# Three of eight experts with 64 slots, both parts of a token in one stationary tile, experts chosen by a register

## The chip, the cores and the metric

The kernel runs on one core of a Trainium2 chip. The number is the device time of one execution in microseconds (us). The engines named below are TensorE (PE, matmuls; PEld is its weight loads), VectorE (DVE), ScalarE (ACT), GpSimd (POOL) and SyncE (SP, which issues the transfers from HBM). Each takes its instructions in a fixed order; between engines there are semaphores.

## The reference

Two layers over 256 tokens of width 1024. The second layer ends in a mixture of experts, and the change is in that part alone:

```python
logits = (a @ w_r).astype(jnp.float32) + b_r.astype(jnp.float32)
top_v, top_i = lax.top_k(logits, TOP_K)          # 2 of 8 experts per token
gates = jax.nn.softmax(top_v, axis=-1)
...
ys = lax.map(lambda args: swiglu(args[0], w1[args[1]], w3[args[1]], w2[args[1]]), (xs, blk_exp))
# swiglu(a, w1, w3, w2) = (silu(a @ w1) * (a @ w3)) @ w2, inner width 2816
```

With the reference's inputs the router sends 47, 66, 93, 32, 81, 113, 59 and 21 tokens to experts 0 to 7.

## The kernel before

All arithmetic is float32. A float32 matmul is made of three faster ones on parts: each operand is split into a high part (rounded to the faster format, `float32r`) and a low part (the rest), and `mm3` (lines 173 to 176) adds high x high, low x high and high x low. The weights are split on the chip: a *unit* is 128 x 2048 floats, 1 MB of HBM, loaded by SP into one of ten raw buffers (`rw`, `rp`, `ra`, `rq`; class `Loads`, issue on line 49). ACT writes the high part (`wh`, line 80), DVE subtracts it from the raw unit (`wl`, line 84), and the raw buffer is free for the next transfer. There are three pairs of high and low buffers for the units of the experts (class `Parts`): `unit()` takes the next unit for TensorE, gives back the pair that TensorE used before it, and issues the splitting of the unit that goes into that pair. A unit of the experts is cast and subtracted in two halves of 1024 columns.

An expert has 11 chunks of 256 inner columns, and a chunk three units: two for w1 and w3 (`up`, 12 matmuls of 512 columns each, result `h`) and one for w2 (`down`, 12 matmuls, accumulated in `y`). Between them stand `act` (silu and product, tile `ga`) and `hidden` (two transposes into `ht`, then the high part `hh` on ACT and the low part `hl` on DVE). Each expert has 128 token slots, which are the 128 columns of the stationary tile. The tokens of a pair of experts are collected by one-hot matmuls (`gather`, during the odd expert before), and the outputs are weighted (`yh`, `yl`) and spread back into the token stream (`xl`, line 1206) in the expert that follows. In chunk g TensorE does `up` of g (with the transposes of g - 1 in its middle) and then `down` of g - 1. The order of all this is written out by hand. At the end a branch repeats an expert for tokens beyond slot 128; with the counts above it isn't taken.

The names of the prediction's steps: `Loads.advance` (45), `Parts.pump` (72), `up`, `act`, `hidden`, `down` (1159 to 1185), and the loop that calls them (1220 to 1272).

Of the kernel before, what the change touches and what calls it, by code (L numbers as in the profile page):

```python
# [34 lines left out]
NCH = FT // 2  # L35
LAM = 0.8 - 0.6 * math.exp(-0.3)


class Loads:
# [6 lines left out]
    def advance(self, most=99):  # L46
        while self.free and self.n < self.limit and most:
            t = self.free.popleft()
            self.nc.sync.dma_start(t, self.aps[self.n])
            self.got[self.n] = t  # L50
            self.n += 1
            most -= 1
# [11 lines left out]
class Parts:  # L64


    def __init__(self, nc, loads, engines, slots):
        self.nc, self.loads, self.engines, self.free = nc, loads, engines, deque(slots)
        self.got, self.n, self.cur, self.spent, self.left, self.holding = {}, 0, 0, [], [], False
        self.limit, self.last_use = len(loads.aps), None  # L70
# [39 lines left out]
    def release(self, most=99):  # L110

        self.holding = False
        keep = [self.spent.pop()] if self.left else []
        for n in self.spent:
            self.free.append(self.got.pop(n))
        self.spent = keep
        self.pump(most)
# [13 lines left out]
def backbone(ctx: ExitStack, tc: tile.TileContext, i, out):  # L131
# [18 lines left out]
    for e in range(NE):  # L150
        for c in range(NCH):
            units += [i["moe"][e, 3 * c], i["moe"][e, 3 * c + 1]]
            if e or c:
                e0, c0 = (e, c - 1) if c else (e - 1, NCH - 1)
                units.append(i["moe"][e0, 3 * c0 + 2])
    units.append(i["moe"][NE - 1, 3 * NCH - 1])
# [6 lines left out]
    def engines(u):  # L163

        if u >= 69:
# [4 lines left out]
    parts = Parts(nc, loads, engines, slots)  # L170
    aloads = Loads(nc, [i["ada"][l, u] for l in range(2) for u in range(24)], ada_slots)
# [722 lines left out]
    def routing(p):  # L894

        iota = p.tile([P, 2, P], F32, name="iota")
        PO.iota(iota.rearrange("p a s -> p (a s)"), pattern=[[1, 2 * P]], base=1, channel_multiplier=0,
                allow_small_or_imprecise_dtypes=True)
# [10 lines left out]
        f = {n: p.tile([P, 2, NE], F32, name=n) for n in ("lg", "rank", "posp", "gate")}  # L909
# [4 lines left out]
        f["cnt"] = p.tile([P, 1 + NE], F32, name="cnt")  # L914
        f["cnti"] = p.tile([P, 1 + NE], mybir.dt.int32, name="cnti")
# [137 lines left out]
    def onehot(t, pr, part):  # L1053

        for n in range(2):
            e = 2 * pr + n
            V.tensor_scalar(oh[t][:, n], r["iota"][:, part], r["posp"][:, t, e:e + 1], None, op0=OP.is_equal)
# [25 lines left out]
    for t in range(2):  # L1083
        onehot(t, 0, 0)
# [8 lines left out]
    def gates():  # L1093
# [5 lines left out]
        V.tensor_copy(r["cnt"][:, 1:], pp)  # L1099
# [7 lines left out]
        V.tensor_reduce(r["cnt"][:, 0:1], r["cnt"][:, 1:], axis=AX.X, op=OP.max)  # L1107
        V.tensor_copy(r["cnti"], r["cnt"])

    def gather():

        xs = [[xlo[:, b * D:(b + 1) * D].rearrange("p (k s) -> p k s", k=KT) for b in range(2)],
              [px.tile([P, KT, P], F32R, name=f"xs{b}", bufs=2) for b in range(2)]]
        late = None

        def low(x, k):
            for n in range(2):
                V.tensor_tensor(out=xs[n][1][:, k], in0=x[:, n], in1=xs[n][0][:, k].bitcast(F32), op=OP.subtract)  # L1120

        for k in range(KT):
# [11 lines left out]
            for n in range(2):  # L1134
                A.copy(xs[n][0][:, k], x[:, n])
# [23 lines left out]

    def up(ps, xs, h, w, ks=range(4)):  # L1160
        for k in ks:
            c = slice(k * T2, (k + 1) * T2)
            mm3(ps, xs[0][:, 4 * h + k], xs[1][:, 4 * h + k], w[0][:, c], w[1][:, c], h == k == 0, h == 1 and k == 3)

    def act(ps):
# [5 lines left out]
    def hidden(g):  # L1171
        pt = pst.tile([P, T], F32, name="ht")
        for f in range(2):
# [7 lines left out]
    def down(y, h, w, first, last):  # L1181
        for f, n in ((0, 0), (1, 0), (0, 1), (1, 1)):
            b = slice(f * P, (f + 1) * P)
            c = slice(f * D + n * T2, f * D + (n + 1) * T2)
            mm3(y[n], h[0][:, b], h[1][:, b], w[0][:, c], w[1][:, c], first and f == 0, last and f == 1)
# [33 lines left out]

    run, got, rets = gather(), {}, {}  # L1220
# [3 lines left out]
    last, res, parted = None, None, deque()  # L1224
    for e in range(NE):
        for c in range(NCH):
            n, pr = e % 2, e // 2
            ps = psh.tile([P, T2], F32, name="h13")
            w = parts.unit()
            for k in range(4):  # L1230
                if e == c == 0:
                    next(run)
                up(ps, got[pr][n], 0, w, [k])
                if k == 1 and last is not None:
                    h = hidden(last[2])
                    if res is not None:
                        parted.extend((m, w, res[2]) for m, w in enumerate(weighted(*res[:2])))
                        res = None
            if e == c == 0:
                next(run)  # L1240
                for _ in range(2):
                    parts.give(1)
                parts.holding = False
            if e == 0 and c == 1:
                gates()
            w = parts.unit()
            up(ps, got[pr][n], 1, w)
            g = act(ps)
            if parted:
                spread(*parted.popleft())  # L1250
            if last is not None:
                e0, c0, _ = last
                if c0 == 0:
                    y = acc()
                down(y, h, parts.unit(), c0 == 0, c0 == NCH - 1)
                if c0 == NCH - 1:
                    gs = rets[e0 // 2][1][:, e0 % 2:e0 % 2 + 1]
                    back = rets[e0 // 2][0][:, e0 % 2]
                    res = y, gs, back
# [126 lines left out]
```

## Time and profile before

| | |
|---|---|
| runs | 1630.42, 1634.49, 1636.94 us; median 1634.49 |
| profiled execution | 1633.3 us, of which the span is 1631.5 |
| experts, by the trace | from about 820 us to the end |
| busy over the span | PE 97%, PEld 80%, DVE 81%, ACT 55%, POOL 3% |
| granted TensorE clock | 0.985 of full speed |
| read from HBM | 397.87 MB, 264 units of the experts among it |

The span runs from the first to the last recorded instruction. A busy share is an average over stages with different limits, so the stage of the experts is looked at by itself. Ends of matmuls are modelled in the records; the distance from start to start of neighbours tells how fast they follow each other.

### The profile page before, as it was taken

Reading aid. Unit: us, or ns where it says so; the run is one execution under the profiler, and the core shown is the slowest. Engines: PE = TensorE matmul, PEld = TensorE weight load, DVE = VectorE, ACT = ScalarE, POOL = GpSimd, SP = SyncE. Lnnn points to the kernel's source line nnn. Section 1 sums busy time; section 2 is a strip of 40 time slices with the busy share of each in tenths; the row PEclk is TensorE's granted clock in tenths of the full one; section 3 lists DMA queues with packets and bytes.
Section 4 is the critical chain, followed back from the end, with each engine's and each line's share of the span. In section 5 each row is a group of like instructions: output and inputs, shape, how many; then the busy total and the mean of one; then the engine's idle time right before and its main releaser. Section 6 shows DMA issues by size and latency. Waiting matters only on the chain. (4 is left out here: it accounts for less than half of the span.)

```text
span 1631.5 us, 20995 instructions
## 1 busy us (share of the span) xinstructions
PE 1584.1 (97%) x7767; PEld 1307.2 (80%) x7767; DVE 1317.6 (81%) x1898; ACT 890.2 (55%) x1241; POOL 44.5 (3%) x157
## 2 busy tenths in 40 slices
PE   9899899999999999999899999999999999999997
PEld 7687689888888898887778888888888888888885
DVE  5888887758648667667578999989999899998986
ACT  3222244222222244445577778777777777877774
POOL 0000000000000002113000000000000000000000
PEclk9899999999999999999989999999999999999999
DMA  9245534545537514322459989999899999999890
GB/s 364 104 161 198 196 123 149 179 137 183 204 130 290 200 53 149 111 78 107 177 192 361 363 322 353 355 351 357 337 345 355 356 342 346 356 350 357 341 358 28
DMA packets 55728, 400.36 MB, mean 245 GB/s; under 512 B 6449, under 2 KB 6481, under 8 KB 7105
## 3 DMA queue, kind: packets, MB, share of 16 engines
q1 hardware_dynamic: 55298, 398.50, 65.0%
q8 instruction: 63, 1.03, 0.2%
q0 software_dynamic: 320, 0.44, 0.2%
q14 instruction: 47, 0.39, 0.1%
HBM read 397.87 MB, written 1.05 MB: 245 GB/s over the span
## 5 line engine op out<-in xcount | busy, mean ns | idle before, releaser
L84 DVE TENSOR_TENSOR wl<-rw,wh 128x1024 fp32r<-128x1024 f32 (+1 forms) x220 | 330.0, 1531 | 80.3 <-ACT wh L80 79.7
L80 ACT CAST wh<-rw 128x1024 fp32r<-128x1024 f32 (+1 forms) x219 | 276.9, 1296 | 63.3 <-PE mm L175 56.4
L174 PE MATMUL mm<-ah,wh 128*128 128x512 f32 (+1 forms) x576 | 222.4, 386 | 5.3 <-ACT ah L314 4.5
L176 PE MATMUL mm<-ah,wl 128*128 128x512 f32 (+1 forms) x576 | 221.2, 384 | 5.2 <-DVE wl L84 5.2
L175 PE MATMUL mm<-al,wh 128*128 128x512 f32 (+1 forms) x576 | 221.5, 384 | 0.0
L84 DVE TENSOR_TENSOR wl<-rp,wh 128x1024 fp32r<-128x1024 f32 (+1 forms) x160 | 192.9, 1246 | 19.7 <-ACT wh L80 19.7
L254 DVE SCALAR_TENSOR_TENSOR junk<-ra,cb 128x1024 bf16<-128x1024 f32 x136 | 166.3, 1223 | 3.3
L80 ACT CAST wh<-rp 128x1024 fp32r<-128x1024 f32 (+1 forms) x160 | 164.9, 1069 | 4.5 <-PE y L176 3.1
L174 PE MATMUL h<-wh,xl 128*128 128x512 f32 x352 | 144.7, 411 | 0.2 <-ACT wh L80 0.2
L175 PE MATMUL h<-wl,xl 128*128 128x512 f32 x352 | 140.9, 400 | 1.8 <-DVE wl L84 1.8
L174 PE MATMUL h<-wh,xs 128*128 128x512 f32 x352 | 142.7, 405 | 0.0
L176 PE MATMUL h<-wh,xl 128*128 128x512 f32 x352 | 140.0, 398 | 0.0
L174 PE MATMUL y<-wh,hh 128*128 128x512 f32 x352 | 138.9, 395 | 0.5 <-ACT hh L1177 0.5
L176 PE MATMUL y<-wh,hl 128*128 128x512 f32 x352 | 139.2, 396 | 0.0
L175 PE MATMUL y<-wl,hh 128*128 128x512 f32 x352 | 139.1, 395 | 0.0
L175 PE MATMUL h<-wl,xs 128*128 128x512 f32 x352 | 139.0, 395 | 0.0
L176 PE MATMUL h<-wh,xs 128*128 128x512 f32 x352 | 139.0, 395 | 0.0
L176 PEld LDWEIGHTS mm<-ah,wl 128*128 128x128 f32 x576 | 110.7, 192 | 27.9 <-DVE wl L84 7.2
L174 PEld LDWEIGHTS mm<-ah,wh 128*128 128x128 f32 x576 | 110.6, 192 | 27.6 <-ACT ah L314 5.3
L84 DVE TENSOR_TENSOR wl<-rq,wh 128x1024 fp32r<-128x1024 f32 x104 | 122.1, 1219 | 8.9 <-ACT wh L80 8.9
L84 DVE TENSOR_TENSOR wl<-ra,wh 128x1024 fp32r<-128x1024 f32 x104 | 122.5, 1220 | 8.2 <-ACT wh L80 6.9
L175 PEld LDWEIGHTS mm<-al,wh 128*128 128x128 f32 x576 | 110.8, 192 | 21.5 <-DVE al L309 0.9
(290 smaller groups left out, 2921.4 us busy)
## 6 DMA issues: line engine op xcount, KB each, us to landing
rw<-moe SPq DMA_DIRECT2D x81, 1024.0 KB, 5.0
rp<-moe SPq DMA_DIRECT2D x79, 1024.0 KB, 5.1
rw<-w SPq DMA_DIRECT2D x61, 1024.0 KB, 4.8
ra<-moe SPq DMA_DIRECT2D x52, 1024.0 KB, 4.9
rq<-moe SPq DMA_DIRECT2D x52, 1024.0 KB, 5.3
ra<-ada SPq DMA_DIRECT2D x44, 1024.0 KB, 4.9
rx<-ada SPq DMA_DIRECT2D x4, 1024.0 KB, 19.7
rp<-w SPq DMA_DIRECT2D x4, 1024.0 KB, 6.3
```

Source lines behind the costliest of these rows:

```text
L80: self.nc.scalar.copy(hi[:, c0], raw[:, c0])
L84: engine.tensor_tensor(out=lo[:, c], in0=raw[:, c], in1=hi[:, c].bitcast(F32), op=OP.subtract)
L174: PE.matmul(ps, wh, xh, start=first, stop=False)
L175: PE.matmul(ps, wh, xl, start=False, stop=False)
L176: PE.matmul(ps, wl, xh, start=False, stop=last)
L254: V.scalar_tensor_tensor(junk, raw[:, a * D:(a + 1) * D], 1.0, cb[:, s], op0=OP.mult, op1=OP.mult, accum_out=m[:, a, s:s + 1])
```

## The change

Experts 2 to 7 are put in an order on the chip, by their numbers of tokens (`places_of`): the three that have the fewest take places 2, 4 and 6 (`FEW`). Since the order is known only on the chip, SP reads it into registers (`choose`) and adds a register to the address of each of the 198 transfers of places 2 to 7.

A place in `FEW` has 64 slots. The high parts of its tokens stand in columns 0 to 63 of one stationary tile and the low parts in 64 to 127, so that a piece of weights takes two matmuls (times the high and the low weights, `two`) instead of three. The result has both parts' products in different partitions; `act` only copies it to SBUF (`hs`), and `hidden` adds the two by a matmul with a folding matrix (`fold`, four matmuls of 64 columns), then does silu, the product (`hg`) and the split. The units of these places are cast and subtracted whole, in one instruction of 2048 columns. In every third chunk (1, 4, 7, 10 of 0 to 10) the second unit isn't split at all (`whole`): TensorE multiplies the raw unit in plain float32, and its raw buffer is given back only when TensorE is done.

For all experts `down` comes one chunk later: chunk g does `up` with its first unit, `down` of g - 2, `hidden` of g - 1, `up` with its second unit, `act`. The units are loaded in that order. An expert's weighting and spreading move by as much. The branch at the end is taken beyond slot 64 for places in `FEW`.

```diff
     def pump(self, most=99, between=None):
-        while self.free and self.n in self.loads.got and self.n < self.limit and most:
+        while self.n in self.loads.got and self.n < self.limit and most and (self.free or self.n in self.whole):
             raw = self.loads.take(self.n)
+            if self.n in self.whole:
+                self.got[self.n] = raw, None
+                self.n += 1
+                continue
...
+    def moe_unit(e, u):
+        if e < 2:
+            return i["moe"][e, u]
+        return lambda: i["moe"][bass.ds(chosen[e - 2], 1), u].rearrange("a p c -> (a p) c")
...
-        if u >= 69:
+        if u >= 69 and u not in few:
             return [(c, [(V, c)]) for c in (slice(0, 1024), slice(1024, U))]
         return [(ALL, [(V, ALL)])]
...
+    def two(ps, x, w, c, first, last):
+        if w[1] is None:
+            PE.matmul(ps, x.bitcast(F32), w[0][:, c], start=first, stop=last)
+        else:
+            for b in range(2):
+                PE.matmul(ps, x, w[b][:, c], start=first and b == 0, stop=last and b == 1)
...
+    def act(ps, few=False):
+        if few:
+            g = px.tile([P, T2], F32, name="hs")
+            A.copy(g, ps)
+            return g
...
+    def hidden(g, few=False):
         pt = pst.tile([P, T], F32, name="ht")
+        if few:
+            for f in range(4):
+                PE.matmul(pt[:, f * H:(f + 1) * H], g[:, f * P:(f + 1) * P], fold, start=True, stop=True)
+            g = px.tile([P, P], F32, name="hg")
+            A.activation(g, pt[:, :P], AF.Silu)
+            V.tensor_tensor(out=g, in0=pt[:, P:], in1=g, op=OP.mult)
+            hb = px.tile([P, T], F32R, name="hh").rearrange("p (f b s) -> p f b s", f=2, b=2)
+            g = g.rearrange("p (f s) -> p f s", f=2)
+            A.copy(hb[:, :, 0], g)
+            V.tensor_tensor(out=hb[:, :, 1], in0=g, in1=hb[:, :, 0].bitcast(F32), op=OP.subtract)
+            return [hb]
...
+    for g, (e, c) in enumerate(chunks):
+        n, pr, few_now = e % 2, e // 2, e in FEW
+        ps = psh.tile([P, T2], F32, name="h13")
+        w = parts.unit()
+        for k in range(4):
...
+            up(ps, got[pr][n], 0, w, [k])
...
+        if g > 1:
+            y = finish(g - 2)
...
+        if g > 0:
+            hids[g - 1] = hidden(acts.pop(g - 1), chunks[g - 1][0] in FEW)
...
+        w = parts.unit()
+        for k in range(4):
+            up(ps, got[pr][n], 1, w, [k])
...
+        acts[g] = act(ps, few_now)
```

What the change does to the order of instructions is shown at expert 2 (place 2 after the change), on three engines. On ACT, one chunk of that expert before (`wh` are casts, `hh` and `ga` belong to the hidden values; what an instruction waits for stands in brackets):

```order
L1167 ACTIVATE ga<-h_8185 128x256 [waits DVE_49,PE_49]
L80 CAST wh_76<-rw_71 128x1024 [waits DMAHW5_49,DVE_49]
L80 CAST wh_76<-rw_71 128x1024 [waits DVE_49]
L80 CAST wh_78<-rp_4396 128x1024 [waits DMAHW6_49,DVE_49,PE_49]
L80 CAST wh_78<-rp_4396 128x1024 [waits DVE_49,PE_49]
L1177 CAST hh<-ht 128x256 [waits DVE_49,PE_49]
```

And on ACT, of the changed kernel, from the end of chunk 2 to the end of chunk 5 of place 2 (`hs` is the copy in `act`, `hg` the silu):

```order
L1251 COPY hs<-h_8242 128x512 [waits PE_49,Activation_49]
L88 CAST wh_74<-rp_4397 128x2048 [waits DMAHW0_49]
L88 CAST wh_76<-ra_70 128x2048 [waits DMAHW1_49,PE_49,Activation_49]
L1264 ACTIVATE hg<-ht 128x128 [waits DVE_49,PE_49]
L1268 CAST hh<-hg 128x2x64 [waits DVE_49]
L88 CAST wh_78<-rw_72 128x2048 [waits DMAHW2_49,Activation_49]
...
L88 CAST wh_74<-rw_73 128x2048 [waits DMAHW7_49,PE_49,Activation_49]
L1264 ACTIVATE hg<-ht 128x128 [waits DVE_49,PE_49]
L1268 CAST hh<-hg 128x2x64 [waits DVE_49]
L88 CAST wh_76<-rp_4396 128x2048 [waits DMAHW0_49]
L1251 COPY hs<-h_8421 128x512 [waits PE_49,Activation_49]
```

The cast `hh` now waits for DVE (the product `hg`), where it waited for TensorE, and one weight cast of each chunk stands behind it. The last five rows are a chunk after an unsplit unit, which has two weight casts instead of three. On DVE, one chunk of that expert before (`wl` are the subtractions of the weights):

```order
L84 TENSOR_TENSOR wl_77<-rp_4395,wh_76 128x1024 [waits DMAHW3_49,Activation_49]
L84 TENSOR_TENSOR wl_77<-rp_4395,wh_76 128x1024 [waits Activation_49]
L84 TENSOR_TENSOR wl_79<-rw_73,wh_78 128x1024 [waits DMAHW4_49,Activation_49]
L84 TENSOR_TENSOR wl_79<-rw_73,wh_78 128x1024 [waits Activation_49]
L1178 TENSOR_TENSOR hl<-ht,hh 128x256 [waits Activation_49]
```

Nothing of ACT waits for `hl` here. On DVE, chunk 3 of place 2 after:

```order
L92 TENSOR_TENSOR wl_75<-rq_6527,wh_74 128x2048 [waits DMAHW4_49,Activation_49]
L92 TENSOR_TENSOR wl_77<-rq_6528,wh_76 128x2048 [waits DMAHW5_49,PE_49,Activation_49]
L1265 TENSOR_TENSOR hg<-ht,hg 128x128 [waits Activation_49]
L1269 TENSOR_TENSOR hh<-hg,hh 128x2x64 [waits Activation_49]
L92 TENSOR_TENSOR wl_79<-rw_71,wh_78 128x2048 [waits DMAHW6_49,Activation_49]
```

The product `hg`, which ACT's `hh` waits for, stands behind two subtractions of 2048 columns. On TensorE, a stretch of chunk 3 of place 2 after: the end of `down`, the fold, and the start of the second `up`.

```order
L1237 MATMUL y_8253<-wh_78,hh 128x512
L1237 MATMUL y_8253<-wl_79,hh 128x512
L1262 MATMUL ht<-fold,hs 128x64 [waits Activation_49]
L1262 MATMUL ht<-fold,hs 128x64 x3
L1237 MATMUL h_8303<-wh_74,xl_5950 128x512 [waits Activation_49]
L1237 MATMUL h_8303<-wl_75,xl_5950 128x512 [waits DVE_49]
```

Each piece of weights has two matmuls where it had three, the fold has taken the place of two transposes, and the second matmul of a unit already needs the low part of the weights.

## Rows read from the trace of the kernel before

**Rows 1.** Windows: length, busy PE, PEld, DVE, ACT, POOL, clock, DMA, GB/s.

```profile
1000.00:1100.00 100.00, 100.00 (x460) 81.27 (x459) 92.20 (x110) 77.09 (x100) 0.00 (x0) 1.00 0.91 352
```

**Rows 2.** TensorE's longest wait from 820 us on: total, times, longest.

```profile
PE h L175 <- DVE wl L84: 1.8, 1, 1.8
```

**Rows 3.** Timeline of TensorE, one chunk of expert 2: start, length, instruction.

```profile
1104.52 0.39 PE L174 MATMUL h<-wh,xl 128*128 128x512 f32 x1
...
1105.69 0.39 PE L176 MATMUL h<-wh,xl 128*128 128x512 f32 x1
...
1106.37 0.40 PE L175 MATMUL h<-wl,xl 128*128 128x512 f32 x1
...
1113.13 0.39 PE L174 MATMUL h<-wh,xl 128*128 128x512 f32 x1
```

**Rows 4.** Timeline of DVE, weighting of the outputs of experts 0, 1, 2.

```profile
935.36 1.40 DVE L1193 SCALAR_TENSOR_TENSOR yl<-y,gs,yh 128x512 fp32r<-128x512 f32 x2
...
1036.01 1.40 DVE L1193 SCALAR_TENSOR_TENSOR yl<-y,gs,yh 128x512 fp32r<-128x512 f32 x2
...
1134.00 1.41 DVE L1193 SCALAR_TENSOR_TENSOR yl<-y,gs,yh 128x512 fp32r<-128x512 f32 x2
```

**Rows 5.** Timeline of TensorE, matmuls in plain float32.

```profile
720.86 1.05 PE L852 MATMUL o<-rp,wT 128*128 128x128 f32 x8
721.66 0.48 PE L174 MATMUL mm<-wh,ah 128*128 128x512 f32 x1
...
805.78 1.85 PE L1029 MATMUL o<-wrg,xl 128*128 128x8 f32 x16
```

**Rows 6.** Groups by form, whole run, ACT.

```profile
L80 ACT CAST wh<-rw 128x2048 fp32r<-128x2048 f32 x63 | 119.4, 1904 | 59.7 <-PE mm L175 56.4 <-PE mm L176 3.3
...
L475 ACT COPY cs<-mm 128x512 f32<-128x512 f32 x8 | 4.6, 579 | 0.0
...
L854 ACT ACTIVATE ojunk<-o 128x128 f32<-128x128 f32 x16 | 4.6, 285 | 6.9 <-PE o L852 6.8
```

**Rows 7.** Timelines of ACT and DVE in the first layer, two stretches.

```profile
287.82 0.62 ACT L564 CAST hh<-cs 128x512 fp32r<-128x512 f32 x1 [6.66 <-DVE cs L563]
288.35 1.91 ACT L80 CAST wh<-rw 128x2048 fp32r<-128x2048 f32 x1
...
341.13 1.91 ACT L80 CAST wh<-rw 128x2048 fp32r<-128x2048 f32 x1 [9.25 <-PE mm L175]
...
343.07 2.29 DVE L84 TENSOR_TENSOR wl<-rw,wh 128x2048 fp32r<-128x2048 f32 x1 [0.83 <-ACT wh L80]
345.28 1.22 DVE L254 SCALAR_TENSOR_TENSOR junk<-ra,cb 128x1024 bf16<-128x1024 f32 x1
```

**Rows 8.** Groups by form, whole run: busy, mean ns | idle before, DVE.

```profile
L84 DVE TENSOR_TENSOR wl<-rw,wh 128x2048 fp32r<-128x2048 f32 x64 | 146.3, 2290 | 67.1 <-ACT wh L80 67.1
...
L1206 DVE SCALAR_TENSOR_TENSOR xl<-g,mod,xl 128x256 f32<-128x256 f32 x64 | 26.5, 479 | 0.1
...
L729 DVE TENSOR_TENSOR qz<-mm,rope 128x128 f32<-128x128 f32 x32 | 7.1, 284 | 6.6 <-ACT qsq L717 6.5
```

**Rows 9.** Timeline of TensorE, second chunk of expert 0.

```profile
834.39 0.69 PE L1174 MATMUL ht<-ident,ga 128*128 128x128 f32 x2 [0.94 <-DVE ga L1168]
```

**Rows 10.** Timeline of TensorE, waits with a slow stretch behind them.

```profile
149.28 0.50 PE L176 MATMUL mm<-ah,wl 128*128 128x512 f32 x1 [1.83 <-DVE wl L84]
...
150.33 0.63 PE L174 MATMUL mm<-ah,wh 128*128 128x512 f32 x1
150.76 0.63 PE L175 MATMUL mm<-al,wh 128*128 128x512 f32 x1
...
153.73 0.39 PE L176 MATMUL mm<-ah,wl 128*128 128x512 f32 x1
```

**Rows 11.** Windows of TensorE: length, busy, clock, DMA, GB/s.

```profile
172.00:176.00 4.00, 1.55 (x7) 1.00 0.00 0
```

**Rows 12.** Windows: the last columns are clock, DMA share and GB/s.

```profile
16.00:20.00 4.00, 4.00 (x20) 4.00 (x21) 3.06 (x8) 2.00 (x4) 0.00 (x0) 1.00 1.01 424
```

More of the change, by code (lines that the diff above doesn't have):

```diff
@@ L35 @@
 NCH = FT // 2
+FEW = (2, 4, 6)
+H = P // 2
 LAM = 0.8 - 0.6 * math.exp(-0.3)
@@ L1184, in down @@
             c = slice(f * D + n * T2, f * D + (n + 1) * T2)
-            mm3(y[n], h[0][:, b], h[1][:, b], w[0][:, c], w[1][:, c], first and f == 0, last and f == 1)
+            a = first and f == 0, last and f == 1
+            if len(h) == 1:
+                two(y[n], h[0][:, f].rearrange("p b s -> p (b s)"), w, c, *a)
+            else:
+                mm3(y[n], h[0][:, b], h[1][:, b], w[0][:, c], w[1][:, c], *a)
     def weighted(y, g):
@@ L1223, in backbone @@
     parts.holding = True
[L1224 to L1239, printed above, removed]
-                next(run)
[L1241 to L1259, printed above, removed]
-            if n == 0 and c == 4:
-                rets[pr] = returns(pr)
-            if n == 1 and e < NE - 1:
-                if c == 1:
-                    for t in range(2):
-                        onehot(t, pr + 1, 0)
-                    run = gather()
-                if 2 <= c < 2 + KT:
-                    got[pr + 1] = next(run)
-            last = e, c, g
@@ L1270, in backbone, with finish @@
-    h = hidden(g)
-    down(y, h, parts.unit(), False, True)
+    res, parted, acts, hids, y = None, deque(), {}, {}, None
+    def finish(g):
+        result = y
+        e, c = chunks[g]
+        if c == 0:
+            result = acc()
+        down(result, hids.pop(g), parts.unit(), c == 0, c == NCH - 1)
+        return result
+    for g, (e, c) in enumerate(chunks):
+        n, pr, few_now = e % 2, e // 2, e in FEW
+        ps = psh.tile([P, T2], F32, name="h13")
+        w = parts.unit()
+        for k in range(4):
+            if g == 0:
+                next(run)
+            up(ps, got[pr][n], 0, w, [k])
+        if g == 0:
+            next(run)
+            for _ in range(2):
+                parts.give(1)
+            parts.holding = False
+        if g > 1:
+            y = finish(g - 2)
+            if chunks[g - 2][1] == NCH - 1:
+                e0 = chunks[g - 2][0]
+                res = y, rets[e0 // 2][1][:, e0 % 2:e0 % 2 + 1], rets[e0 // 2][0][:, e0 % 2]
+        if g > 0:
+            hids[g - 1] = hidden(acts.pop(g - 1), chunks[g - 1][0] in FEW)
+        if g == 1:
+            gates()
+        if g == 2:
+            places_of()
+            V.tensor_tensor(out=fold, in0=ident[:, :H], in1=ident[:, H:], op=OP.add)
+        if g == 4:
+            choose()
+        w = parts.unit()
+        for k in range(4):
+            up(ps, got[pr][n], 1, w, [k])
+            if k == 1 and res is not None:
+                parted.extend((m, v, res[2]) for m, v in enumerate(weighted(*res[:2])))
+                res = None
+        acts[g] = act(ps, few_now)
+        if parted and c > 1:
+            spread(*parted.popleft())
+        if n == 0 and c == 4:
+            rets[pr] = returns(pr)
+        if n == 1 and e < NE - 1:
+            if c == 1:
+                for t in range(2):
+                    onehot(t, pr + 1)
+                run = gather(pr + 1)
+            if 2 <= c < 2 + KT:
+                got[pr + 1] = next(run)
@@ L1272, in backbone @@
+    y = finish(g - 1)
+    hids[g] = hidden(acts.pop(g))
+    y = finish(g)
     for n, w in enumerate(weighted(y, rets[3][1][:, 1:2])):
```

116 lines of the change are left out of this document (85 added, 31 removed).

## The prediction

> **What bounds the kernel now.** The windows come first. From 1000 us on, in the stage of the experts, TensorE is busy all the time at the full clock (2.4 GHz), DVE 92%, ACT 77%, and the transfers bring 352 GB/s [rows 1]. Busy TensorE time is modelled, so the list of waits is read next: from 820 us to the end TensorE's longest wait is 1.8 us, and it comes once [rows 2]. Then the timeline of one chunk: five matmuls of 512 columns start in 1.17 us, 0.234 us each; two transposes take 0.21 us more (0.68 us between two matmuls that stand two apart, less 2 x 0.234); the chunk takes 8.61 us [rows 3], which is its 36 matmuls (8.42) and its transposes. So TensorE's instructions are the bound. The weightings of the outputs mark the experts: expert 1, in which tokens are gathered, takes 100.65 us, expert 2, in which none are, 98.0 [rows 4]. Places 2, 4 and 6 are of the second kind, and 98.0 us each is what the change can shorten.
>
> **What TensorE saves.** Two matmuls for three: 12 fewer in each of 11 chunks, 132 x 0.234 = 30.9 us an expert. Back come two things. In four chunks a unit is multiplied in plain float32. Four such matmuls of 128 columns took 0.80 us [rows 5], so one of 512 columns 0.80 and a unit 3.2, where eight split ones take 1.87: 1.33 more, 5.3 an expert. The fold is four float32 matmuls, which the trace records as eight; sixteen records with 8 columns took 1.85 us [rows 5], so the fold takes 0.92 against 0.21 for the transposes: 7.8 an expert. TensorE alone would need 98.0 - 30.9 + 5.3 + 7.8 = 80.2 us, a gain of 17.8 for each of three experts.
>
> **What the splitting allows.** ACT and DVE have to split a unit in the time of eight matmuls. A cast of 2048 columns takes 1.90 us [rows 6], its subtraction follows 1.94 us after the cast's start, and DVE goes on 2.21 us after that [rows 7]. DVE alone: 29 units x 2.21, 22 small ones of 0.28 for product and low part, eight of 0.48 for spreading [rows 8], 1.4 for weighting [rows 4], together 75.5 us. That would fit as well. What doesn't is the order. In a chunk with three splits DVE stands at: two subtractions (4.42), the product `hg` (0.28). ACT's `hh` waits for that product (0.03), takes 0.28 by the nearest row, a pass over 128 columns [rows 6], of which the next cast hides 0.09, as a cast behind a shorter one starts 0.53 us after it where that one takes 0.62 [rows 7]; then comes the third cast, and 1.94 later the third subtraction. That is 4.42 + 0.31 + 0.20 + 1.94 = 6.87. In these 2.1 us DVE has only the small low part to do. The next chunk's first cast stands behind the copy `hs` (0.58 [rows 6], less 0.09): its subtraction starts 1.82 + 0.49 = 2.31 after the third. The chunk takes 9.18 us, more than the 8.61 of before.
>
> A chunk with two casts takes 2.21 less, 6.97. It follows the float32 unit, and its first cast goes into the pair that TensorE has then just used: down, fold, float32 unit and up (1.87 + 0.92 + 3.2 + 1.87) after the third subtraction, which is 0.7 later than ACT comes to it. Three chunks: 2 x 9.18 + 6.97 + 0.7 = 26.0, and TensorE has only 20.9 us of work in them. Chunks 1 to 9 are three such rounds, 78.1. Chunk 10 already splits the next expert's units in halves (8.4 by the same sum), chunk 0 still has the hidden values of the old kind, whose `hh` waits for nothing on DVE (7.3). Spreading adds 8 x 0.39 on DVE, weighting and the copies behind `returns` about 1.6 on the two engines (an estimate; they were beside TensorE's work before). Together 78.1 + 15.7 + 3.1 + 1.6 = 98.5 us against 98.0. **TensorE's 17.8 us are gone: it waits for weights instead**, +0.5 an expert. The bounds of this term: 80.2 us (TensorE alone) and 105 (9.18 in all eleven chunks and the 4 us beside them). I take the chain, since every piece of it but `hg` and `hh` is a row of the same form.
>
> **The other experts.** Places 3, 5 and 7 keep 36 matmuls. At the start of a place of `FEW` TensorE has about one split unit in hand, at its end none: the smaller place gains some 2 us, and the expert behind it has to earn its lead again. There TensorE's first chunk is 0.94 shorter than DVE's work wants, its exchange for `hg` still comes once (about 0.4), and in the two chunks that spread, DVE has 1.6 more and only 8% of 8.61 to spare (0.9 each); with the weighting some 4 us. Net +2 for each of three, bounds -2 (no lead lost) and +6.
>
> **The rest.** In expert 0 the wait of 0.94 us for `ga` [rows 9] goes, since `hidden` comes later; the fourteen small DVE instructions that rank the experts come in its third chunk and cost some of it again: -1, bounds -4 and +3. SP's 198 transfers with a register cost a few register operations each, which no row shows: between nothing and as long as a unit may take, 2.9 us (1.05 MB at 352 GB/s [rows 1]), before they are seen; ten raw buffers stand between, and I take nothing. If SP took longer, the transfers would set the pace. The raw buffer of a float32 unit is free later, one of ten. The new constants on POOL are made once, far ahead of their use.
>
> **Sum.** 3 x 0.5 + 3 x 2 - 1 = +6.5 us on the profiled execution's 1633.3 (span 1631.5 and 1.8 around it): 1639.8. The median of the runs shown lies 1.2 higher, so **1641 us**. Less than 0.5% (8 us: 1626.3 to 1642.7) can't be told from no change.
>
> **Rivals.**
>
> *TensorE keeps the pace.* If the small `hg`, `hh` exchange costs less than worked out, or splits run far enough ahead after each float32 unit, the expert falls towards 80.2: 1634.5 - 3 x 17.8 = 1581; half of it gives 1608. For it: DVE's own work is only 75.5 us. Against it: in-order queues, and only three pairs.
>
> *TensorE's clock falls, on the other side.* In two chunks of three TensorE now waits 2 us or more for the low part of a w2 unit. Behind a wait of 1.83 us at 149 us, itself a second wait, it ran at half the clock (1.2 GHz): eight matmuls in the 3.4 us to 153.73, 0.43 us each [rows 10]: 1.5 us lost. But a window with 1.55 us of work in 4 kept the full clock [rows 11]. If each of the 22 waits brings such a stretch and all of it reaches the end, that is +33: 1674. It decides once a stretch delays the fold by more than the 1.7 us that `hg` has in hand behind two subtractions; my sum takes nothing for that. The worst end, half the clock in all 33 chunks, is TensorE's 41.8 us for 26.0 in eleven rounds, +174, which the window speaks against. The Trainium skill ("TensorE: Matmul & The Clock Gate", Part 1) calls the slow clock the default, which activity releases; by it the waits alone would bring it on. The rows show both, so it gets a share, not the forecast.
>
> *The transfers set the pace.* If the 352 GB/s of this stage [rows 1] were all that can be had, 33 units of 1.05 MB would take 98.3 us, and nothing could come below today's 98.0: about 1634. Against it: 424 GB/s in the start [rows 12], 81.6 us for 33 units. The Trainium skill ("DMA: Bandwidth & Descriptors", Specifications) gives about 358 GB/s as one core's limit to HBM; by that an expert would need an estimated 96.7 us, and the time would be about 1631. The start's row is above that limit, so the row decides.
>
> *More than 64 tokens.* If a place of `FEW` had more, the branch would repeat it, unoverlapped: about 200 us by cast, subtraction and matmuls of 33 units one after the other. The counts of places 2, 4 and 6 would be 59, 32 and 21, so it isn't taken.
>
> **Chances.** The chain with its neighbours 0.55 (1641, own range 1626 to 1660; of it 0.03 faster, 0.27 same, 0.25 slower); TensorE's pace, wholly or in part, 0.20 (1581 to 1622, faster); the clock 0.17 (1655 to 1700, slower); the transfers 0.06 (same); the branch 0.02. Faster 0.23, same 0.33, slower 0.44. The range is 1600 to 1682: half of the second case and a third of the clock's are left out.
>
> **What would show it.** Right: in places 2, 4 and 6 TensorE waits for `wl` and `wh` some 15 us an expert, DVE waits for ACT's cast about 2 us in each chunk right behind `hg`, three chunks take about 26 us, and the weightings stand some 97 to 100 us apart. The split of the sum: 8 matmuls in 1.87 us, fold 0.92, float32 unit 3.2. Wrong: TensorE without waits there and experts of 80 to 85 us; or a granted clock below 0.9 in these stretches; or DVE and ACT waiting for transfers, with a rate at 352 GB/s or below; or experts 3, 5 and 7 longer than 105 us.

## The result, and the profile after

The changed kernel takes 1652.28 us (median of 4 runs, 1648.0 to 1656.26), the kernel before beside it 1634.36 (4 runs, 1630.42 to 1636.94): ratio 1.0111, 95% interval 1.0079 to 1.0144, so it is slower, by 1.1%. The profiled execution has a span of 1650.7 us, 19.2 more than before. All of the difference arises among the experts, and the weightings of their outputs show where. Timeline of DVE after, outputs of places 0 to 4 (start, length, instruction; they answer to [rows 4]):

```profile
938.96 1.40 DVE L1295 SCALAR_TENSOR_TENSOR yl<-y,gs,yh 128x512 fp32r<-128x512 f32 x2
...
1043.79 1.40 DVE L1295 SCALAR_TENSOR_TENSOR yl<-y,gs,yh 128x512 fp32r<-128x512 f32 x2
...
1145.44 1.41 DVE L1295 SCALAR_TENSOR_TENSOR yl<-y,gs,yh 128x512 fp32r<-128x512 f32 x2
...
1251.64 1.40 DVE L1295 SCALAR_TENSOR_TENSOR yl<-y,gs,yh 128x512 fp32r<-128x512 f32 x2
...
1349.13 1.40 DVE L1295 SCALAR_TENSOR_TENSOR yl<-y,gs,yh 128x512 fp32r<-128x512 f32 x2
```

Place 2 takes 101.65 us and place 4 97.49, where 98.0 stood before: the 17.8 us that TensorE saves in each are gone, as forecast. Places 1 and 3, which have nothing of the new form, take 104.83 and 106.20 where it was 100.65. That was not forecast for place 1 at all.

TensorE now waits; its busy time is modelled, so part 1 of the page after tells only the shares of the engines, and the waits below are read next:

```profile
PE 1553.3 (94%) x7569; PEld 1264.6 (77%) x7569; DVE 1281.9 (78%) x1799; ACT 866.1 (52%) x1163; POOL 44.9 (3%) x162
```

TensorE's longest sums of waits after, from 820 us to the end (waiting instruction <- what it waits for: total, times, longest). Before, the longest stood alone with 1.8 us [rows 2]:

```profile
PE y L1237 <- DVE wl L92: 27.3, 18, 1.8
PE g L1197 <- DVE xl L1308: 11.9, 6, 3.0
PE y L1237 <- DVE yl L1295: 5.0, 3, 1.7
```

The first row is the small places' `down`, waiting for the low part of a w2 unit. The second is the gathering of tokens (`g`, in places 1, 3, 5), waiting for the spreading of outputs (`xl`). The same view of DVE:

```profile
DVE wl L92 <- ACT wh L88: 94.8, 102, 2.2
```

and of ACT:

```profile
ACT hh L1268 <- DVE hg L1265: 45.2, 33, 3.1
ACT xl L1206 <- DVE gx L1204: 30.1, 16, 4.9
```

ACT's `hh` waits for DVE's `hg` in each of the 33 small chunks, DVE's subtraction for ACT's cast: each engine stands while the other works. One chunk of place 4 shows the exchange. Timeline of ACT after:

```profile
1269.19 3.70 ACT L88 CAST wh<-rq 128x2048 fp32r<-128x2048 f32 x2
1273.96 0.28 ACT L1264 ACTIVATE hg<-ht 128x128 f32<-128x128 f32 x1 [1.06 <-PE ht L1262]
1277.34 0.30 ACT L1268 CAST hh<-hg 128x128 fp32r<-128x128 f32 x1 [3.10 <-DVE hg L1265]
1277.55 1.90 ACT L88 CAST wh<-rw 128x2048 fp32r<-128x2048 f32 x1
```

and of DVE:

```profile
1272.63 4.48 DVE L92 TENSOR_TENSOR wl<-rq,wh 128x2048 fp32r<-128x2048 f32 x2
1277.03 0.28 DVE L1265 TENSOR_TENSOR hg<-ht,hg 128x128 f32<-128x128 f32 x1
1277.67 0.29 DVE L1269 TENSOR_TENSOR hh<-hg,hh 128x128 fp32r<-128x128 f32 x1 [0.36 <-ACT hh L1268]
1279.47 2.29 DVE L92 TENSOR_TENSOR wl<-rw,wh 128x2048 fp32r<-128x2048 f32 x1 [1.51 <-ACT wh L88]
```

ACT has `hg`'s silu ready at 1274.24 and stands 3.10 us until DVE is through two subtractions; then DVE stands 1.51 us until the third cast is there.

### The profile page after: what moved, and what is told of

Same layout as the page of the kernel before. It is cut to its first block, busy times and chain, and to the rows that moved or that the text cites. A ratio compares the mean times of both kernels' runs of the same rounds, so it can differ in the third digit from the quotient of the medians.

```text
span 1650.7 us, 20590 instructions
## 1 busy us (share of the span) xinstructions
PE 1553.3 (94%) x7569; PEld 1264.6 (77%) x7569; DVE 1281.9 (78%) x1799; ACT 866.1 (52%) x1163; POOL 44.9 (3%) x162
## 5 line engine op out<-in xcount | busy, mean ns | idle before, releaser
L92 DVE TENSOR_TENSOR wl<-rp,wh 128x1024 fp32r<-128x1024 f32 (+1 forms) x122 | 174.9, 1465 | 35.0 <-ACT wh L88 31.4
L88 ACT CAST wh<-rp 128x1024 fp32r<-128x1024 f32 (+1 forms) x122 | 147.4, 1244 | 4.4 <-issue 1.7
L92 DVE TENSOR_TENSOR wl<-ra,wh 128x1024 fp32r<-128x1024 f32 (+1 forms) x81 | 114.5, 1444 | 20.2 <-ACT wh L88 19.4
L92 DVE TENSOR_TENSOR wl<-rq,wh 128x1024 fp32r<-128x1024 f32 (+1 forms) x87 | 124.3, 1476 | 6.8 <-ACT wh L88 6.4
L88 ACT CAST wh<-rq 128x1024 fp32r<-128x1024 f32 (+1 forms) x87 | 104.2, 1256 | 0.0
L88 ACT CAST wh<-ra 128x1024 fp32r<-128x1024 f32 (+1 forms) x81 | 96.7, 1230 | 2.7 <-PE h L202 2.0
L1237 PE MATMUL h<-wh,xl 128*128 128x512 f32 x216 | 89.9, 416 | 0.0
L1237 PE MATMUL h<-wl,xl 128*128 128x512 f32 x216 | 86.0, 398 | 2.3 <-DVE wl L92 2.3
L201 PE MATMUL y<-wl,hh 128*128 128x512 f32 x220 | 87.1, 396 | 1.1 <-DVE wl L92 1.1
L200 PE MATMUL y<-wh,hh 128*128 128x512 f32 x220 | 87.4, 397 | 0.5 <-ACT hh L1275 0.5
```

The costliest lines, as they stand in the source:

```text
L88: self.nc.scalar.copy(hi[:, c0], raw[:, c0])
L92: engine.tensor_tensor(out=lo[:, c], in0=raw[:, c], in1=hi[:, c].bitcast(F32), op=OP.subtract)
L200: PE.matmul(ps, wh, xh, start=first, stop=False)
L201: PE.matmul(ps, wh, xl, start=False, stop=False)
L1237: PE.matmul(ps, x, w[b][:, c], start=first and b == 0, stop=last and b == 1)
```

## Each expert in each kernel

To place every difference, the distance from an expert's last `act` (last `ga` or `hs` on ACT) to that of the expert before it was taken from each profiled execution's timeline (us); the medians are those of the timed runs. Places 2, 4, 6 are small in all but the first and fourth rows.

| kernel | 1 | 2 | 3 | 4 | 5 | 6 | 7 | median |
|---|---|---|---|---|---|---|---|---|
| before | 100.6 | 98.0 | 100.7 | 98.0 | 100.6 | 98.0 | 96.7 | 1634.4 |
| after | 104.3 | 102.3 | 105.6 | 98.6 | 103.7 | 101.0 | 95.4 | 1652.3 |
| e_static | 104.2 | 98.6 | 103.6 | 101.0 | 105.7 | 99.5 | 95.4 | 1651.2 |
| e_nofew | 104.3 | 98.0 | 105.8 | 98.0 | 104.3 | 97.9 | 96.4 | 1645.8 |
| e_split | 105.8 | 104.3 | 106.8 | 103.7 | 106.8 | 103.6 | 96.6 | 1666.6 |
| e_clock | 105.8 | 99.2 | 105.2 | 99.3 | 105.3 | 99.3 | 95.0 | 1649.8 |
| e_cast | 105.8 | 97.4 | 103.3 | 97.5 | 101.9 | 97.4 | 93.2 | 1637.3 |
| e_mid | 104.3 | 88.5 | 105.2 | 88.5 | 103.7 | 88.5 | 95.2 | 1615.2 |
| e_half | 105.8 | 91.1 | 103.3 | 91.2 | 103.3 | 91.1 | 95.1 | 1621.6 |
| e_gather | 101.8 | 101.9 | 101.6 | 100.3 | 101.6 | 103.2 | 95.4 | 1643.0 |
| e_quart | 100.3 | 113.1 | 99.6 | 112.0 | 99.7 | 112.0 | 95.5 | 1671.3 |
| e_quart2 | 100.3 | 102.8 | 99.7 | 99.1 | 99.2 | 102.1 | 95.1 | 1635.4 |
| e_best | 100.3 | 92.5 | 99.0 | 92.5 | 99.1 | 92.5 | 95.3 | 1611.6 |
| e_best2 | 100.3 | 85.7 | 99.0 | 85.6 | 99.0 | 85.7 | 95.3 | 1590.9 |

After against before: places 1, 3, 5 together +11.7, places 2, 4, 6 together +7.9, place 7 -1.3, the rest (start, place 0, tail) +0.9, which makes the 19.2 of the spans. Two theories were to be told apart: that the small places' chain between DVE and ACT costs it all, or that places 1, 3 and 5 have a loss of their own. All ratios below are against the kernel before, on the same chip; all edits are made in the changed kernel.

## Experiments

**e_nofew: no small places, all else as changed.**

```diff
-FEW = (2, 4, 6)
+FEW = ()
```

> No place has 64 slots (FEW empty): the ranking, the addresses by register, and the new order of the loop stay, all experts do three matmuls with 128 slots and no unit is multiplied unsplit. Theory (the three small places cost 8 us against before, the later spreading of the others about 10): 1642-1645, experts 2, 4 and 6 at 98.0 us again, experts 1, 3 and 5 at 103-105. Rival (the addresses by register, or the new order, cost something everywhere): experts 2, 4 and 6 stay above 100 and the time at 1650 or more. Second rival (it is all in the small places): 1634.

Measured: 1645.76 us, ratio 1.0078 (1.0058 to 1.0097). Places 2, 4, 6 are back at 98.0; places 1, 3, 5 stay 4 us long. So a loss of about 12 us has nothing to do with the small places, and the new order and register addresses cost the even places nothing.

**e_static: the same transfers from fixed addresses**, experts in their own order; the registers are still read, and the tokens meet the weights of other experts, so only its time is used.

```diff
-        if e < 2:
-            return i["moe"][e, u]
-        return lambda: i["moe"][bass.ds(chosen[e - 2], 1), u].rearrange("a p c -> (a p) c")
+        return i["moe"][e, u]
```

> The transfers of places 2 to 7 have fixed addresses (the weights of experts 2 to 7 in their own order, so that the ranked tokens meet the wrong experts); the registers are still read. Theory (a register in a transfer's address costs nothing that is seen): within 3 us of 1652, transfers as long and as late as before. Rival (SP's register operations, or a transfer that starts later, cost time in all six places): 1645 or less, and shorter waits of DVE and ACT for DMA.

Measured: 1651.2 us, 1.0113 (1.0096 to 1.013), the same as with registers: a register in the address of 198 transfers costs nothing that is seen. The rest of the instructions is that of the changed kernel, and here place 2 takes 98.6 and place 4 101.0, the other way round: which small place is the longer one changes from execution to execution.

**e_gather: the gathering one chunk later.** Spreading moved one chunk with `down`; gathering did not. Before, only the second of the two chunks that spread shared a chunk's end with a step of gathering; now both do. And before, the twelve matmuls of `down` stood between the two on TensorE; now gathering follows spreading at once. Timelines of TensorE and ACT before, expert 3:

```profile
1146.60 0.28 PE L1203 MATMUL g<-back,yl 128*128 128x256 f32 x1
1146.72 0.40 PE L174 MATMUL y<-wh,hh 128*128 128x512 f32 x1
...
1149.52 0.28 PE L1126 MATMUL g<-oh,nh 128*128 128x256 f32 x1
...
1152.16 0.30 ACT L1135 CAST xl<-gx 128x128 fp32r<-128x128 f32 x1 [3.92 <-DVE gx L1133]
```

Timeline of the changed kernel in place 3 (all engines, some rows left out):

```profile
1155.35 1.65 DVE L1308 SCALAR_TENSOR_TENSOR xl<-g,mod,xl 128x256 f32<-128x256 f32 x4
1156.27 0.39 PE L1197 MATMUL g<-oh,nh 128*128 128x256 f32 x1 [3.01 <-DVE xl L1308]
...
1157.05 0.55 DVE L1204 TENSOR_SCALAR gx<-g,mod 128x256 f32<-128x256 f32 x1
1157.11 0.63 PE L201 MATMUL h<-wl,xs 128*128 128x512 f32 x1
...
1157.62 0.24 ACT L1206 CAST xl<-gx 128x64 fp32r<-128x64 f32 x1 [4.88 <-DVE gx L1204]
...
1157.97 1.99 ACT L88 CAST wh<-rw 128x1024 fp32r<-128x1024 f32 x2
1159.05 2.36 DVE L92 TENSOR_TENSOR wl<-rw,wh 128x1024 fp32r<-128x1024 f32 x2 [1.46 <-ACT wh L88]
```

Spreading and gathering take their accumulators `g` from the same two PSUM buffers. Gathering's matmul stands 3.01 us until DVE has emptied one; DVE's `gx` follows; ACT's cast of the gathered tokens has stood 4.88 us for it, with the next weight casts queued behind; and TensorE goes on at half its clock (0.63 a matmul, starts 0.43 apart). ACT's wait is hardly new: it was 3.92 before. TensorE's is: its six waits for `g` make 11.9 us in places 1, 3 and 5, where it had none of this kind before.

```diff
-            if c == 1:
+            if c == 2:
                 for t in range(2):
                     onehot(t, pr + 1)
                 run = gather(pr + 1)
-            if 2 <= c < 2 + KT:
+            if 3 <= c < 3 + KT:
```

> The gathering of the next pair's tokens (and its one-hot tiles) starts one chunk later, in chunks 3 to 10 instead of 2 to 9, so that it shares one chunk with the spreading instead of two, as in the kernel before. Theory (gather and spread share two PSUM buffers, and a gather's matmul waits for xl): chunks 3 and 4 of experts 1, 3 and 5 (12-15 and 11.5 us) fall by 3-4 us together, the kernel by 9-12, to 1640-1643. Rival (DVE simply has too much to do there, wherever it stands): less than 4 us, 1648 or more.

Measured: 1643.03 us, 1.0054 (1.0036 to 1.0073). Places 1, 3, 5 fall to 101.6 to 101.8, 8.5 us in all, and TensorE's waits for `g` to 6.7 us. The median falls by 9; the profiled execution, at 1650.3 the longest of five, by 2 only, since place 0 and the small places came out longer in it. The meeting of the two is the loss of these places, and one meeting without `down` in between still costs them some 3 us against before.

**e_quart and e_quart2: spreading in four quarters, one accumulator a chunk**, over chunks 2 to 5; in e_quart2 also `returns` (the transposed gates of the pair) in chunk 7 of the even expert.

```diff
-    def spread(n, w, back):
+    def spread(n, w, back, ks=(0, 2)):
-        for k in range(4 * n, 4 * n + 4, 2):
+        for k in (4 * n + k for k in ks):
...
-                parted.extend((m, v, res[2]) for m, v in enumerate(weighted(*res[:2])))
+                parted.extend((m, v, res[2], (k0,)) for m, v in enumerate(weighted(*res[:2])) for k0 in (0, 2))
...
-        if n == 0 and c == 4:
+        if n == 0 and c == 7:
             rets[pr] = returns(pr)
```

(The last piece is e_quart2's alone.)

> The kernel after, with the spreading of a smaller expert's outputs in four quarters over chunks 2 to 5 of the expert behind it (one accumulator of the pair that spreading and gathering share, and four units of work on DVE, in each chunk) instead of in two halves over chunks 2 and 3; the gathering stays where it is, in chunks 3 to 6. Theory (two chunks of experts 1, 3 and 5 are long because a chunk's spreading asks for two accumulators of that pair and for DVE, while gathering asks for them too): chunk 3 falls from 12.5 to 15 us to about 10, chunk 2 and 4 a little, chunks 5 and 6 may grow by some tenths; experts 1, 3 and 5 take 101 to 102 us each, and the time is 1638 to 1644 us. Rival (it is gathering alone, or the length that DVE lacks in any case): chunks 3 and 4 together stay near 25 us, or what they lose comes back in chunks 5 and 6; 1648 us or more.

Measured: 1671.29 us, 1.0217 (1.0198 to 1.0235), a miss. Places 1, 3, 5 did fall, to 99.6 to 100.3, further than expected; but the small places grew by 11 to 13 us, nearly all in one chunk of 20 us. ACT's waits in place 4 of e_quart:

```profile
ACT back L1221 <- PE g L1305: 12.4, 1, 12.4
```

`back` is one buffer; its next content is made in chunk 4, and the last quarter, in chunk 5, still reads the old one. ACT stands in order, and no weight is cast for 12.4 us.

> Spreading in quarters over chunks 2 to 5, and the transposed gates of the pair (`returns`) made in chunk 7 of the even expert instead of chunk 4. Theory (in the run before, ACT's copy into the single buffer `back` stood 12 us behind the last quarter's matmuls, which still read it, and held up the weight casts queued behind it): chunk 5 of the smaller experts falls from 20 us to 8 or 9, these experts take 98 to 102 us as with the change alone, experts 1, 3 and 5 stay at 99.5 to 100.5; the time is 1634 to 1643 us. Rival (the quarters themselves cost the smaller experts some 10 us): 1655 us or more.

Measured: 1635.41 us, 1.0018 (0.9996 to 1.004), no different from before. The wait for `back` is gone, places 1, 3, 5 stay at 99.2 to 100.3. Timeline of e_quart2, the same chunk of place 3:

```profile
1147.82 0.28 PE L1197 MATMUL g<-oh,nh 128*128 128x256 f32 x1
...
1150.57 0.86 DVE L1308 SCALAR_TENSOR_TENSOR xl<-g,mod,xl 128x256 f32<-128x256 f32 x2
...
1151.92 0.25 ACT L1206 CAST xl<-gx 128x64 fp32r<-128x64 f32 x1 [3.98 <-DVE gx L1204]
```

One of the two accumulators is free now, so gathering starts before DVE has emptied the other, and from 820 us on TensorE waits for `g` in gathering nowhere. ACT still stands 3.98 us for `gx`, behind DVE's `xl`, and the place loses nothing by it: what cost was TensorE's own wait for the accumulators. Against after, these three places are 14.4 us shorter and the median 16.9: the collision is the greater part of what the change cost (11.7 of 19.2 us).

**e_cast: the third weight cast ahead of the silu and `hh`.** If `hh` holds up the cast, putting the cast first should help.

```diff
-            hids[g - 1] = hidden(acts.pop(g - 1), chunks[g - 1][0] in FEW)
+            few_was = chunks[g - 1][0] in FEW
+            if few_was:
+                w = parts.unit()
+            hids[g - 1] = hidden(acts.pop(g - 1), few_was)
...
-        w = parts.unit()
+        w = w or parts.unit()
```

> The third weight cast of a chunk of FEW is issued ahead of the silu, hh and hg instead of behind them; nothing else moves. Theory (DVE and ACT wait for each other behind hg, which sets the pace): DVE's chunk falls from 9.2 to about 7.2 us, so a round of three chunks goes from 26.2 to 21-22 us, near TensorE's own 20.9; the three experts go from about 100.6 to 83-87 us, the kernel from 1652 to 1600-1615. Rival (TensorE, its clock, or the transfers set the pace there): rounds stay at 25-27 us and the time within 8 us of 1652; if only the transfers stand next, 33 units need at least 82 us and DVE waits for DMA.

Measured: 1637.32 us, 1.0026 (1.0016 to 1.0037); small places 97.4 to 97.5. A miss by over 20 us: the wait only moved. Timelines of e_cast, ACT:

```profile
1268.10 0.28 ACT L1264 ACTIVATE hg<-ht 128x128 f32<-128x128 f32 x1
1271.57 0.30 ACT L1268 CAST hh<-hg 128x128 fp32r<-128x128 f32 x1 [3.19 <-DVE hg L1265]
```

and DVE:

```profile
1269.05 2.29 DVE L92 TENSOR_TENSOR wl<-rw,wh 128x2048 fp32r<-128x2048 f32 x1
1271.25 0.28 DVE L1265 TENSOR_TENSOR hg<-ht,hg 128x128 f32<-128x128 f32 x1
...
1274.68 2.29 DVE L92 TENSOR_TENSOR wl<-rp,wh 128x2048 fp32r<-128x2048 f32 x1 [2.42 <-ACT wh L88]
```

The product now stands behind three subtractions, `hh` behind it, and the next chunk's first cast behind `hh`: DVE waits 2.42 us there instead.

**e_mid: the same cast between the silu and `hh`**, so that DVE's product stays ahead of its third subtraction, and ACT has the cast to do while it is made.

```diff
             A.activation(g, pt[:, :P], AF.Silu)
             V.tensor_tensor(out=g, in0=pt[:, P:], in1=g, op=OP.mult)
+            second.append(parts.unit())
...
-        w = parts.unit()
+        w = second.pop() if second else parts.unit()
```

> In the places of FEW the chunk's third weight cast stands between the silu and hh on ACT, and its subtraction between hg and the low part on DVE; nothing else moves. After the run with the cast ahead of the silu (the wait stayed, as hs and the next cast stood behind hh, which stood behind three subtractions) the theory is: what costs is any weight cast that stands behind hh while hh waits for a product that stands behind subtractions. Here hh waits only for a product that DVE does while ACT casts. Expected by it: DVE's chunk 7.2 us, a round of three chunks 21-22.5 us (TensorE's own work 20.9), places 2, 4 and 6 at 84-89 us, the kernel 1605-1618. Rival (some other wait takes its place at once, as in that run, or TensorE's clock does): rounds at 24 us or more, the kernel 1630 or more.

Measured: 1615.19 us, 0.989 (0.9874 to 0.9907); small places 88.5. Timeline of ACT in e_mid:

```profile
1271.35 0.28 ACT L1266 ACTIVATE hg<-ht 128x128 f32<-128x128 f32 x1 [1.29 <-PE ht L1264]
1271.53 1.91 ACT L88 CAST wh<-rw 128x2048 fp32r<-128x2048 f32 x1
1273.33 0.30 ACT L1271 CAST hh<-hg 128x128 fp32r<-128x128 f32 x1
```

`hh` has no wait left. Nothing has changed but the order, so the chain between DVE and ACT was what held the small places at 98. (Their granted clock is 1.00 here, as in e_cast; the part of the gain that is the clock's is told at e_clock.)

**e_half: the small places' units in halves**, as before the change: DVE can start when half a unit is cast.

```diff
-        if u >= 69 and u not in few:
+        if u >= 69:
```

> The units of FEW are cast and subtracted in two halves of 1024 columns, as in the other places. Theory: the wait behind hg becomes about 0.85 us shorter, as DVE can start after half a cast; a round of three chunks falls from 26.2 to about 24 us, the kernel by 20-25, to 1627-1632. Rival (TensorE or the transfers set the pace): no change, or a little slower for the more instructions.

Measured: 1621.62 us, 0.9925 (0.9906 to 0.9944), better than expected; small places 91.1. Shorter links shorten the chain even with a second set of instructions.

**e_split: no unit in plain float32.**

```diff
-    parts.whole = set(whole)
+    parts.whole = set()
```

> No unit is multiplied in plain float32: all units of FEW are split. Theory (DVE and ACT set the pace): all chunks become 9.2 us instead of 9.2, 9.2 and 7.7, a round 27.6, the three experts 4-5 us longer each, the kernel 1662-1668. Rival (TensorE's float32 unit of 3.5 us is on the path): a round gets shorter by up to 1.7 us and the kernel is 1640-1650.

Measured: 1666.62 us, 1.0207 (1.019 to 1.0224), as expected. With three splits in every chunk the small places take 103.6 to 104.3, with a granted clock of 0.93 to 0.95 in them; the prediction's upper bound for this was 105.

**e_clock: eight small matmuls, whose result nothing reads, ahead of `down` in each chunk of the small places**, to keep TensorE at work while it would wait.

```diff
+        if few_now and len(got[pr][n]) == 3:
+            fill = pst.tile([P, T], F32, name="ht")
+            for k in range(8):
+                PE.matmul(fill, got[pr][n][2][:, k], oh[0].rearrange("p n s -> p (n s)"), start=True, stop=True)
```

> Eight needless matmuls of 256 columns (0.12 us each) ahead of down in the places of FEW, where TensorE waits some 2 us for weights; their result goes to a buffer that is overwritten. Theory of the clock (the longer rounds of places 2 and 6, 27-28 us against 26.2 in place 4, are TensorE at 1.2 GHz behind its waits): the clock stays at full speed, all rounds become 26-26.5 us and the kernel 4-7 us faster, 1645-1648. Rival (the clock costs nothing on the path): 1650-1656.

Measured: 1649.81 us, 1.0098 (1.008 to 1.0117), between the two. Windows of e_clock, one in place 2 (length, busy time of PE, PEld, DVE, ACT, POOL, granted clock, DMA share, GB/s):

```profile
1034.00:1126.00 92.00, 87.47 (x437) 68.29 (x437) 71.42 (x61) 62.23 (x63) 0.00 (x0) 1.00 0.92 352
```

and of after, two in place 2, each with one wait of 1.83 us for `wl`, and one of place 4:

```profile
1057.00:1069.00 12.00, 10.17 (x42) 7.60 (x42) 10.12 (x10) 6.47 (x6) 0.00 (x0) 0.86 0.78 275
...
1105.00:1117.00 12.00, 10.17 (x47) 7.74 (x45) 8.74 (x8) 8.12 (x8) 0.00 (x0) 1.00 0.93 369
...
1236.00:1326.00 90.00, 78.70 (x352) 58.64 (x351) 70.82 (x60) 61.46 (x62) 0.00 (x0) 0.98 0.93 355
```

At the full clock all three small places take 99.3, together 4.1 us less than after, where two of them above all had stretches at the lower clock. The filling has a price of its own: in chunk 0, where TensorE does not wait, it takes 0.95 us, from the start of the next row to that of the `down` behind it at 1029.41:

```profile
1028.46 1.11 PE L1354 MATMUL ht<-oh,xl 128*128 128x256 f32 x8
```

Without it the three places would stand at an estimated 98.3, as near to the 98.6 of place 4 after, and the clock would be worth some 7 us in the small places. The median fell by 2.5 only, since places 1, 3 and 5 came out 2.7 longer in the profiled execution (their chunk 3 takes between 12.5 and 14.9 us in the traces of all kernels that keep the collision); the intervals of the two kernels overlap. That the clock lengthens the small places is shown; what it is worth in the whole kernel's time is not settled. Against those 98.3, e_mid's 88.5 leave some 10 us a place to the chain alone.

**e_best and e_best2: e_mid, e_half and the quarters together**; e_best2 with `returns` in chunk 7.

> Three edits together: the third weight cast of a chunk between silu and the cast of hh, the float32 units in halves, and spreading in quarters. Theory (the chain between DVE and ACT sets the pace of the smaller experts, and the shared accumulators that of experts 1, 3 and 5): the smaller experts fall from 98.6 to 102 us to 82 to 86, bounded by TensorE's own 80; experts 1, 3 and 5 take about 101; in all 1588 to 1604 us. Rival (transfers: 33 units an expert at 352 GB/s need 98 us, at 424 GB/s 82): smaller experts stay at 88 us or more, DVE and ACT wait for raw buffers, and the time is 1605 us or more.

Measured: 1611.55 us, 0.9869 (0.9852 to 0.9885), a miss: the wait for `back` again, 9.8 us in each small place.

> The three edits together, and `returns` in chunk 7. Theory: chunk 5 of the smaller experts falls from 15.0 to about 8.8 us, so these take about 86 us each, 18 us less in all than the run before: 1589 to 1599 us. Rival (what is gained there is lost to the next wait, since DVE and ACT have no slack in the chunk): 1603 us or more.

Measured: 1590.91 us (1590.29 to 1592.11), ratio 0.9745 (0.9731 to 0.9759), the fastest of all: 41.8 us below the kernel before on the same chip. TensorE's first row of waits in e_best2, from 820 us on, and the window of place 2:

```profile
PE y L1237 <- DVE hh L1272: 7.1, 9, 1.2
```

```profile
1027.00:1105.00 78.00, 75.51 (x352) 57.24 (x350) 71.35 (x86) 63.23 (x88) 0.00 (x0) 1.00 1.00 404
```

The small places take 85.65 us; TensorE is busy 97% of the window (87% in the window of place 4 after, where [rows 1] have 100%), and the transfers are busy all of it, though no engine waits for one there. Whether they would allow a shorter place was not tried.

## Why the prediction was right, and where it was not

The forecast was 1641 and slower as the likeliest side; measured were 1652, within the range. The mechanism in the small places held; the sum was too small, +6.5 forecast against +19.2 in the profiled execution, and the greater part of the slowdown, 11.7 us, has a cause that the prediction did not name. That the time came out on the forecast side is luck in part: without that cause, in e_quart2, it is no different from before.

**The splitting.** Right in mechanism and size. Rounds of three chunks were worked out at 26.0; in place 4, the one with nearly the full clock, the two rounds without spreading take 26.2 and 26.1 (chunks 5 to 7 and 8 to 10), and the expert 98.6 against the 98.5 of the sum. (In the prediction's own division, chunk 0, three rounds and chunk 10, it is 7.0, 28.6, 27.7, 26.0 and 9.2, with the spreading and weighting in the first two rounds. The weightings, which fall into the next expert, stand 101.7, 97.5 and 100.4 apart for the three small places.) The waits were taken too long: TensorE is idle 11.3 us in the window of place 4, where 15 an expert were named. The exchange behind `hg` is there row by row: from its end at 1277.31 to the third subtraction DVE has 2.16 us, with only the low part to do, where 2.1 was said. e_mid, e_half and e_split, edits of this chain, move the small places to 88.5, 91.1 and 104; their clock in these places is 1.00, 0.98 and 0.93 to 0.95, so a part of the difference between them is the clock's.

**TensorE's own terms.** The float32 unit was taken at 3.2 us, the fold at 0.92. Timeline of TensorE after, two stretches:

```profile
1046.55 1.00 PE L1262 MATMUL ht<-fold,hs 128*128 128x64 f32 x8
1047.36 0.48 PE L1237 MATMUL h<-wh,xl 128*128 128x512 f32 x1
...
1301.47 3.65 PE L1234 MATMUL h<-rp,xl 128*128 128x512 f32 x8
1304.56 0.79 PE L1237 MATMUL h<-wh,xl 128*128 128x512 f32 x1
```

From start to the next start that is 0.81 and 3.09. (A plain float32 matmul stands as two records.) The 80.2 us that TensorE alone would need are thus somewhat high: by 4 x 0.11 and 11 x 0.11, 1.7 us. They were not the bound here.

**The other experts: the step that failed.** The prediction priced spreading as DVE's own time in two chunks, some 4 us in an expert behind a small one, and took 2 us off each small place for the lead it starts with. Neither is what happens. Place 1, with no small place ahead, pays as much as 3 and 5, and e_nofew has the loss without any small place. The moved step meets gathering at two shared accumulators, now with no `down` between the two, and TensorE stands there itself, 11.9 us in places 1, 3 and 5; ACT's and DVE's waits behind it are not the cause, as e_quart2 keeps ACT's without the loss. The prediction said itself that weighting and spreading move with `down`; it did not ask what stands in the chunk into which they move. The 2 us of lead do not show from `act` to `act`: place 4 would have come to 96.5. The prediction had named experts 3, 5 or 7 above 105 us as a sign against it, and place 3 with 105.6 is one.

**The clock.** Taken at nothing. Behind waits like those of [rows 10] some stretches ran at 1.2 GHz, three in place 2, one in place 4 and two in place 6. Timeline of TensorE after, place 4:

```profile
1289.41 0.50 PE L1237 MATMUL y<-wl,hh 128*128 128x512 f32 x1 [1.82 <-DVE wl L92]
...
1290.28 0.63 PE L1237 MATMUL y<-wh,hh 128*128 128x512 f32 x1
1290.71 0.63 PE L1237 MATMUL y<-wl,hh 128*128 128x512 f32 x1
...
1291.99 1.75 PE L1262 MATMUL ht<-fold,hs 128*128 128x64 f32 x8
```

Most of the waits of this length brought no such stretch (the clock of place 4 is 0.98 on the whole). Place 2 had rounds of 28.6 and 27.4, place 6 of 27.5 and 27.3, and the two carry the rest of the +7.9. The prediction had named a granted clock below 0.9 in these stretches as a sign against it, and the window with 0.86 is one. So the rival was true in a small share: some 7 us, not the +33 of a stretch behind every wait. The Trainium skill ("TensorE: Matmul & The Clock Gate", Part 1) has the slow clock as the default that activity releases; the trace agrees that idling can bring it back. That the waits alone would do so, as the prediction read it, does not hold: two windows of 12 us in place 2, with the same wait and the same 10.17 us of work, had 0.86 and 1.00.

**The other rivals.** TensorE keeping the pace did not come about, though a change of order alone brings the small places to 88.5. Transfers do not set the pace at 352 GB/s: e_best2 draws 404 over 78 us. The Trainium skill ("DMA: Bandwidth & Descriptors", Specifications) puts one core's limit to HBM at about 358 GB/s; the measurement is above it and decides, as [rows 12] did. (A unit at 352 GB/s is 3.0 us, not the 2.9 that the prediction has as a bound; nothing hangs on it.) The branch was not taken (no such instructions stand at the end). Expert 0 and the ranking came to +0.4 with the start, where -1 was taken.

## What to carry to other kernels

When instructions of one engine wait in order for another's, look for the place at which each engine stands while the other works, and slip a long independent instruction into it: e_mid moves one cast ahead of one instruction and gains 37 us against after, while the same cast moved ahead of one more gains 15 (in both with the small places at the full clock). When a step is moved by a stage, list what already stands in the stage it moves into, which buffers both use, single buffers too (`g` here, `back` in e_quart), and what stood between the two that gave the buffers time to empty (`down` here). A saving on the engine that bounds the kernel is worth only what the feeding engines leave of it, and it comes out when their exchange is mended.

## What the hardware showed

Transfers of 1 MB units held 404 GB/s for 78 us with the DMA engines busy all the time, 15% over the 352 of [rows 1], so that rate was demand and not a limit. Eight small matmuls a chunk that compute nothing kept TensorE's granted clock at 1.00 in all three small places, where it was 0.95, 0.98 and 0.96 without them; where TensorE would not have waited, they cost it 0.95 us.
